# A two-layer hybrid decoder trunk in fp32 on one core: transposes at the borders of the MLP handed out as deferred work, and the opening rebuilt

## The chip, the core and the metric

The kernel runs on one core of a Trainium2 chip. The core has a matrix engine (TensorE, PE in the profile; its weight loads are PEld), a vector engine (VectorE, DVE), a scalar engine (ScalarE, ACT), GpSimd (POOL) and a sync engine (SP) that here only issues transfers. Each engine works through its own instructions in their program order and waits at an instruction until what that needs is there. The metric is device time in microseconds (us), less is better. A change of under 0.2% (5 us) can hardly be told from none here.

## The reference

Two layers over h, 256 rows (tokens) by 2048:

```
u = rms_norm(h, norm_mix_pre);  proj = u @ w_in
mix = concat(nsa_mixer(...), rglru_mixer(...), gla_mixer(...))
h = h + rms_norm(mix @ w_out, norm_mix_post)
u = rms_norm(h, norm_mlp_pre)
h = h + rms_norm(square(relu(u @ w_up)) @ w_down, norm_mlp_post)
h = h + sigmoid(h @ w_ple_gate) * (p[i] @ w_ple)
```

## The kernel before

**Two words for one fp32 number.** Every fp32 product is made of three passes over rounded operands. `split` makes the two words: ScalarE rounds to `hi` (CAST), VectorE makes the rest, `lo` = x - hi. A product is then `uh*wh + uh*wl + ul*wh`, in this order in `form_a`; so the first two passes of a block need only the hi word of the activations and the third needs their lo word, which VectorE makes.

**Weights** come as a stream of units of 512 KB, each 128x1024 in SBUF. `ensure(i)` issues the transfer of unit i into one of four `raw` buffers and splits it into one of eight `hi`/`lo` pairs; the products call it NBUF = 8 units ahead, so their code puts one `lo<-raw,hi` on VectorE for every unit used.

**Activations** are multiplied in transposed form. `to_t` transposes a 128x512 block on TensorE, four 128x128 pieces into one bank of the two-bank ring `tr`, and splits the bank in two halves into two units of the tile set `u` (ScalarE `u<-tr`, then VectorE `u<-tr,u`, twice). The 256 rows are two halves, hf = 0 and 1, with four blocks m of 512 columns each.

**Projections** run in `form_a` (activations stationary, both halves share the weight units; with grp = 4 it takes four units for hf 0, then the same four for hf 1) or `form_b` (weights stationary). When a half is finished, its evacuation function runs (`ev_o2`, `ev_dn`, ...).

**Borders.** Two per layer matter here. At the *up border* the last block of the output projection (`o2`, n = 3) is evacuated: norm, `h` updated (`stt`, L153), multiplied by the gain of the next norm into `t` (L153 too), transposed into `u2`. Products of `ple(0)` and `ple(1)` follow (12 each, they need no norm), then `up`, which reads `u2`. At the *gate border* the last block of `w_down` (`dn`, r = 3, n = 3) is evacuated the same way, without the gain, into `u3`; `ple(2)`, `ple(3)` follow, then `pg`, which reads `u3`. The rsqrt of a norm is a `pow` on POOL (L298).

**Order.** A scheduler decides the order on each engine; `tc.high_priority()` puts instructions ahead, `tc.issue_after(x)` puts them behind x. `self.bg` holds generators of background work: `pump` advances them as products are issued, `later` is a transposition that waits for some us of products, `flush` and `drain` run them to their end.

**Opening** (`run`). The gain of the first norm is spread over 128 partitions by four products with a row of ones into four PSUM banks (`gbc`); VectorE multiplies each block of x by it, and then it is transposed. `vw` and `vs` are the first two projections, `c` the third; two small transposes of a gate input `z` (L504) stand ahead of `c`.

Of the kernel before, what the change touches and what calls it, by code (L numbers as in the profile page):

```python
# [10 lines left out]
F32 = mybir.dt.float32  # L11
# [7 lines left out]
P = 128  # L19
D = 2048  # L20
T = 256
# [10 lines left out]
NBUF = 8  # L32
# [68 lines left out]
class Trunk:  # L101
    def __init__(self, ctx, tc, a, depth, dbg=None):
        self.tc, self.nc, self.a, self.depth, self.dbg = tc, tc.nc, a, depth, dbg
        self.n = 0
        pool = lambda name, **k: ctx.enter_context(tc.tile_pool(name=name, bufs=1, **k))
        self.sb = pool("sb")
        self.ps = pool("ps", space=PSUM)
        self.cst()
        self.stream = []
        self.loaded = []  # L110
        self.bg = []
        self.nrm = [None, None]
        self.par = []
        self.credit = 0.0


# [33 lines left out]
        self.nc.vector.tensor_tensor(out, a, b, op=op)  # L150

    def stt(self, out, a, s, b, op0=ALU.mult, op1=ALU.add):
        self.nc.vector.scalar_tensor_tensor(out, a, s, b, op0=op0, op1=op1)  # L153

    def ts(self, out, a, s1, s2=None, op0=ALU.mult, op1=ALU.add):
        if s2 is None:
# [24 lines left out]
    def ensure(self, i):  # L181
        nc = self.nc
        while len(self.loaded) <= min(i, len(self.stream) - 1):
# [18 lines left out]
                self.split(hv[:, :, 256:320], lv[:, :, 256:320], gz)  # L202
            self.loaded.append((hi, lo))

    def pump(self, us):
# [20 lines left out]
    def form_a(self, base, nu, k0, ut, evac, grp=1, kpu=2, w=512, ring=None, pre=None):  # L226
        accs = [(ring or self.acc)() for _ in range(2)]
        self.ensure(base)
        for g in range(0, nu, grp):
            us = range(g, min(nu, g + grp))  # L230
            for hf in range(2):
                if hf and g == 0 and pre:
                    pre()
                for u in us:
                    self.ensure(base + u)
                    hi, lo = self.loaded[base + u]
                    for k in range(kpu):
                        kt = k0 + kpu * u + k
                        uh, ul = ut.get(kt, hf * 128, hf * 128 + 128)
                        wh, wl = hi[:, k * w:k * w + w], lo[:, k * w:k * w + w]  # L240
                        last = u == nu - 1 and k == kpu - 1
                        o = accs[hf][:, 0:w]
                        self.mm(o, uh, wh, u == 0 and k == 0, False)
                        self.mm(o, uh, wl, False, False)
                        self.mm(o, ul, wh, False, last)
                    if hf:
                        self.ensure(base + u + NBUF)
                    self.pump(0.72 * kpu * w / 1024)
                if g + grp >= nu:
                    evac(hf, accs[hf])  # L250
# [51 lines left out]
        j = self.t2()  # L302
        self.actf(j, src, AF.Square, accum_out=dst)

    def to_t(self, src, n, hf, ut):
# [3 lines left out]
        bv = b.rearrange("p (k t) -> p k t", k=4)  # L309
        sl = slice(hf * 128, hf * 128 + 128)  # L310
# [5 lines left out]
    def later(self, us, src, n, hf, ut):  # L316
        while us > 0:
            us -= 1.3
            yield 1.3
        self.to_t(src, n, hf, ut)  # L320

    def flush(self):
        for g in list(self.bg):
# [139 lines left out]
    def layer(self, i, ut):  # L463
# [6 lines left out]

        rf = self.rfac
        self.form_a(B("vw"), 4, 0, ut, lambda hf, acc: self.actf(v[:, hf, 1], acc[:, 0:256], AF.Copy, scale=rf(0, hf)),
                    4 if i else 2, 4, 256, pre=self.flush)
        if i == 0:
            self.cst2()
        gt = self.st([P, 2, 48], "gt", 1)
# [21 lines left out]
                    self.rr[:, None, 0:2, None].to_broadcast([P, 8, 2, 4]))  # L498
            self.rrow()
        self.slr = slr  # L500
        gzt = self.st([16, T], "gzt", 1)
# [6 lines left out]
        kcu = self.unit()  # L508
        kc = kcu.rearrange("p (s c t) -> p s c t", s=2, c=2)
        for x in range(2):  # L510
            self.form_b(B("c", x), 4, ut, None, dst=kcu[:, x * 512:x * 512 + 512])
        self.params(rows)
        cm = {}
        self.bg.append(self.compress(kcu, kc, wk, cm))
# [132 lines left out]
        def finish_norm():  # L647


# [25 lines left out]
        for r in range(4):  # L675
            hid = self.new_ut()
            for c in range(4):
                def ev_up(b, t):
                    self.stt(t, t, 0.0, t, op0=ALU.max, op1=ALU.mult)
                    u = hid.u[2 * c + b]  # L680
                    self.split(u[:, :, 0], u[:, :, 1], t.rearrange("p (k t) -> p k t", k=2))
                if r == 0 and c == 0:
                    def ev_up0(hf, acc):
                        rl, sq = self.t2(), self.t2()
                        self.actf(rl, acc, AF.Relu)
                        self.tt(sq, rl, rl)
# [10 lines left out]
            for n in range(4):  # L697
                def ev_dn(hf, acc):
# [3 lines left out]
                    elif r < 3:  # L702
                        self.tt(yc, acc, yc, ALU.add)
                    else:
                        with self.tc.high_priority():
                            post(hf, n, acc, gpost, y, ss)
                            if n == 3:
                                rs = self.rstd(ss[hf], epsc[hf])
                                for m in range(4):
                                    h = self.h[hf][m]  # L710
                                    self.stt(h, self.col(y[hf], m), rs, h)
# [34 lines left out]
                if n == 3:  # L746
                    self.pre_norm(hf, ss[hf])
        for n in range(4):
            self.form_a(B("pg", n), 8, 0, u3, ev_pg, GRP if n in (0, 3) else 1)
        return None if last else u4  # L750


# [400 lines left out]
    def run(self):  # L1153
# [3 lines left out]
        ut = self.new_ut()  # L1157


        ones = self.sb.tile([1, P], F32, name="ones")  # L1160
        self.nc.vector.memset(ones, 1.0)
        gbc = [self.sc(), self.sc(), self.acc(), self.acc()]
        for k in range(2):
            row = self.unit()[0:1]
            self.nc.scalar.dma_start(row, a["norm_mix_pre"][0:1, k * 1024:k * 1024 + 1024])
            for n in range(2):
                self.mm(gbc[2 * k + n], ones, row[:, n * 512:n * 512 + 512], True, True)
        both = []
        for hf in range(2):
            for n in range(4):  # L1170
                self.dma(self.h[hf][n], a["x"][0, hf * 128:hf * 128 + 128, n * 512:n * 512 + 512])
            if hf == 0:
                self.dma(self.id_, a["cst"][:, C_ID:C_ID + P])

            with ExitStack() as q:
                for b in both:
                    q.enter_context(self.tc.issue_after(b.ins))
                for n in range(4):
                    t = self.t2()
                    self.tt(t, self.h[hf][n], gbc[n])  # L1180
                    both = self.to_t(t, n, hf, ut)
                ss = self.sm(4)
                for n in range(4):
                    self.sumsq(self.h[hf][n], ss[:, n:n + 1])
            with self.tc.issue_after(both[0].ins), self.tc.issue_after(both[1].ins):
                self.ensure(2 * hf)
                both = self.parts
                self.ensure(2 * hf + 1)
            self.pre_norm(hf, ss)
        for i in range(self.depth):  # L1190
            ut = self.layer(i, ut)

# [32 lines left out]
```

## Time and profile before

| | |
|---|---|
| median of three runs | 2486.48 us (2484.9 to 2487.35) |
| the profiled execution | 2484.42 us, span 2482.6 us |
| TensorE busy | 2461.9 us (99% of the span) |
| VectorE, ScalarE busy | 1535.0 us (62%), 1289.7 us (52%) |
| transfers | 451.15 MB, mean 182 GB/s |

TensorE is the engine that sets the time; the other engines matter where TensorE waits for them.

### The profile page before, as it was taken

Reading aid. Unit: us, or ns where it says so; the run is one execution under the profiler, and the core shown is the slowest. Engines: PE = TensorE matmul, PEld = TensorE weight load, DVE = VectorE, ACT = ScalarE, POOL = GpSimd, SP = SyncE. Lnnn points to the kernel's source line nnn. Section 1 sums busy time; section 2 is a strip of 40 time slices with the busy share of each in tenths; the row PEclk is TensorE's granted clock in tenths of the full one; section 3 lists DMA queues with packets and bytes.
Section 4 is the critical chain, followed back from the end, with each engine's and each line's share of the span. In section 5 each row is a group of like instructions: output and inputs, shape, how many; then the busy total and the mean of one; then the engine's idle time right before and its main releaser. Section 6 shows DMA issues by size and latency. Waiting matters only on the chain.

```text
span 2482.6 us, 33799 instructions
## 1 busy us (share of the span) xinstructions
PE 2461.9 (99%) x12962; PEld 2081.8 (84%) x12962; DVE 1535.0 (62%) x2123; ACT 1289.7 (52%) x2002; POOL 29.7 (1%) x42
## 2 busy tenths in 40 slices
PE   8999999999999999999999999999999999999999
PEld 7888888888888888888888788888888888888887
DVE  5776767754555555656657767676546546555564
ACT  5686655554443443445556866655544434444452
POOL 0000000000000000000000000000000000000000
PEclk9999999999999999999999999999999999999999
DMA  7644446656656656565675445456566565565653
GB/s 229 194 139 136 141 165 200 188 185 195 191 190 193 189 188 196 190 206 184 193 201 166 131 139 160 156 186 204 188 196 189 191 194 188 189 194 190 207 186 120
DMA packets 286086, 451.15 MB, mean 182 GB/s; under 512 B 32955, under 2 KB 107715, under 8 KB 285925
## 3 DMA queue, kind: packets, MB, share of 16 engines
q1 hardware_dynamic: 285920, 448.98, 56.7%
q8 instruction: 102, 1.67, 0.3%
q14 instruction: 60, 0.48, 0.1%
q10 hardware_dynamic: 4, 0.01, 0.0%
HBM read 446.84 MB, written 2.10 MB: 181 GB/s over the span
## 4 chain that ended last, share of the span: by engine, by line
PE 94%; DVE 2%; ACT 2%; DMA 1%; issue 0%; POOL 0%; SPq 0%; DVEq 0%; ACTq 0%
PE acc L164 63%; PE sc L164 15%; PE tr L164 14%; PE tr L916 1%; PE tr L308 1%; DMA raw<-in_w_in_dram 1%; ACT t L161 1%; DVE lo L147 1%; ACT hi L147 1%; POOL sm L298 0%; DVE u L150 0%; DVE h L153 0%; DVE u L153 0%; DMA raw<-in_w_up_dram 0%; DVE t L153 0%
## 5 line engine op out<-in xcount | busy, mean ns | idle before, releaser
L147 DVE TENSOR_TENSOR lo<-raw,hi 128x1024 fp32r<-128x1024 f32 (+1 forms) x832 | 1007.4, 1213 | 792.1 <-ACT hi L147 787.3
L147 ACT CAST hi<-raw 128x1024 fp32r<-128x1024 f32 (+1 forms) x832 | 866.4, 1043 | 987.1 <-PE acc L164 578.2
L164 PE MATMUL acc<-hi,u 128*128 128x512 f32 (+2 forms) x2944 | 902.2, 384 | 3.5 <-ACT hi L147 3.4
L164 PEld LDWEIGHTS acc<-hi,u 128*128 128x128 f32 x2944 | 547.6, 189 | 109.0 <-ACT hi L147 4.0
L164 PE MATMUL acc<-lo,u 128*128 128x512 f32 (+2 forms) x1472 | 563.5, 383 | 1.4 <-DVE lo L147 1.4
L164 PE MATMUL acc<-u,hi 128*128 128x512 f32 x1920 | 491.3, 395 | 0.0
L164 PEld LDWEIGHTS acc<-u,hi 128*128 128x128 f32 x1920 | 344.4, 189 | 65.3 <-issue 3.1
L164 PEld LDWEIGHTS acc<-lo,u 128*128 128x128 f32 x1472 | 277.6, 189 | 52.5 <-DVE lo L147 1.9
L164 PEld LDWEIGHTS acc<-u,lo 128*128 128x128 f32 x1920 | 262.2, 190 | 18.7
L164 PE MATMUL acc<-u,lo 128*128 128x256 f32 x1920 | 269.3, 283 | 0.0
L164 PE MATMUL sc<-u,hi 128*128 128x512 f32 x512 | 139.7, 394 | 0.0
L164 PE MATMUL tr<-u,hi 128*128 128x512 f32 x512 | 137.3, 390 | 0.0
L164 PE MATMUL sc<-hi,u 128*128 128x512 f32 x384 | 119.3, 389 | 0.0
L164 PE MATMUL tr<-hi,u 128*128 128x512 f32 x384 | 119.2, 389 | 0.0
L164 PEld LDWEIGHTS tr<-u,hi 128*128 128x128 f32 x512 | 96.1, 188 | 21.4
L164 PEld LDWEIGHTS sc<-u,hi 128*128 128x128 f32 x512 | 88.5, 190 | 11.9
L164 PEld LDWEIGHTS sc<-u,lo 128*128 128x128 f32 x512 | 78.3, 189 | 9.9
L164 PEld LDWEIGHTS tr<-hi,u 128*128 128x128 f32 x384 | 72.1, 188 | 15.0
L164 PEld LDWEIGHTS sc<-hi,u 128*128 128x128 f32 x384 | 72.1, 188 | 14.8
L164 PE MATMUL tr<-u,lo 128*128 128x256 f32 x512 | 82.3, 283 | 0.0
L164 PE MATMUL sc<-u,lo 128*128 128x256 f32 x512 | 81.3, 282 | 0.0
L161 ACT ACTIVATE t<-sc,sm,slr 128x128 f32<-128x128 f32 (+1 forms) x128 | 63.9, 506 | 22.0 <-DVE sm L150 22.0
(195 smaller groups left out, 1753.7 us busy)
## 6 DMA issues: line engine op xcount, KB each, us to landing
raw<-in_w_up_dram SPq DMA_DIRECT2D x256, 512.0 KB
raw<-in_w_down_dram SPq DMA_DIRECT2D x256, 512.0 KB
raw<-in_w_in_dram SPq DMA_DIRECT2D x168, 512.0 KB
raw<-in_w_out_dram SPq DMA_DIRECT2D x64, 512.0 KB
raw<-in_w_ple_gate_dram SPq DMA_DIRECT2D x64, 512.0 KB
raw<-in_w_in_dram SPq DMA_DIRECT2D x16, 256.0 KB
raw<-in_w_ple_dram SPq DMA_DIRECT2D x8, 512.0 KB
h<-in_x_dram SPq DMA_DIRECT2D x8, 256.0 KB
```

The costliest lines, as they stand in the source:

```text
L147: return self.nc.scalar.copy(hi, src), self.nc.vector.tensor_sub(lo, src, hi.bitcast(F32))
L161: self.nc.scalar.activation(out, a, f, **k)
L164: self.last = self.nc.tensor.matmul(out, l, r, start=start, stop=stop, skip_group_check=True)
L308: self.nc.tensor.transpose(b[:, k * 128:k * 128 + 128], src[:, k * 128:k * 128 + 128], self.ident)
L916: nc.tensor.transpose(b[:, x * 128:x * 128 + 128], pe[:, x * 128:x * 128 + 128], self.ident)
```

## The change

1. **Opening.** The gain is loaded as 16 rows of 128, transposed once, and used as a scalar for each partition after the transposition, so x is transposed as it lands; the four products with ones go. The transposes of the second half become background work between the first products; its sums of squares stand behind the splits of units 2 and 3. Two products without use stand ahead of the first projection.
2. **Up and gate border.** The transposes of both halves are no longer issued in the evacuation function, with its high priority, but handed to `later`. `until` finishes those of hf 0 ahead of the first product that reads them, `flush` those of hf 1 inside `form_a`. After the first `stt` of a half, the next four calls of `ensure` are issued behind it (`hold`, `fetch`).
3. **`z`.** Its two transposes and their copy stand behind the products of `c`.

```
+    def fetch(self, i):
+        if not self.hold:
+            self.ensure(i)
+            return
+        with self.tc.issue_after(self.hold[0]):
+            self.ensure(i)
...
-                        self.ensure(base + u + NBUF)
+                        self.fetch(base + u + NBUF)
...
+    def until(self, ut):
+        for g, u in self.due:
+            if u is ut:
+                self.drain(g)
+        self.due = []
...
-                        self.stt(h, self.col(y[hf], m), r, h)
+                        q = self.stt(h, self.col(y[hf], m), r, h)
+                        if m == 0:
+                            self.hold = [q.ins, 4]
                         t = self.t2()
                         self.stt(t, h, nr[:, 1:2], self.col(gpre, m), op0=ALU.mult, op1=ALU.mult)
-                        self.to_t(t, m, hf, u2)
+                        self.bg.append(self.later(1.3 if m else 3.9, t, m, hf, u2))
...
-                    self.form_a(B("up", r, c), 8, 0, u2, ev_up0, GRP)
+                    self.until(u2)
+                    self.form_a(B("up", r, c), 8, 0, u2, ev_up0, GRP, pre=self.flush)
...
-                                    self.to_t(h, m, hf, u3)
+                                    self.bg.append(self.later(1.3 if m else 2.6, h, m, hf, u3))
...
-        gbc = [self.sc(), self.sc(), self.acc(), self.acc()]
...
+        g16, gt = self.unit()[0:16, 0:P], self.sm(16)
+        self.nc.scalar.dma_start(self.id_, a["cst"][:, C_ID:C_ID + P])
+        self.nc.scalar.dma_start(g16, a["norm_mix_pre"][0].rearrange("(k p) -> k p", p=P))
+        b = self.tr()
+        self.nc.tensor.transpose(b[:, 0:16], g16, self.ident[0:16, 0:16])
+        self.nc.vector.tensor_copy(gt, b[:, 0:16])
...
+                    both = self.to_t(self.h[0][n], n, 0, ut, gt[:, 4 * n:4 * n + 4])
...
+                hi = self.loaded[0][0]
+                for _ in range(2):
+                    self.mm(self.sc(), hi[:, 0:P], hi[:, 0:512], True, True)
...
+        def other():
+            for n in range(4):
+                with self.tc.issue_after(first[0].ins), self.tc.issue_after(first[1].ins), \
+                        self.tc.issue_after(self.last.ins):
+                    self.both = self.to_t(self.h[1][n], n, 1, ut, gt[:, 4 * n:4 * n + 4])
+                yield 0.7
+        self.bg.append(other())
```

**What moves on VectorE at the up border of layer 0.** The rows are instructions in their order on the engine, `out<-in`; `h_65` to `h_68` are the blocks of hf 0 and `h_69` to `h_72` those of hf 1, `t_` their multiples by the gain, `lo_` weights, `u_..<-tr_` the lo word of a transposed block. Line numbers are those of the program listed (L153 before is L155 after, L147 is L149). Before, the first split of a transposed block is the sixth row from the first `h`:

```order
L153 SCALAR_TENSOR_TENSOR h_65<-u_3497,sm_4196,h_65 128x512
L153 SCALAR_TENSOR_TENSOR h_66<-u_3497,sm_4196,h_66 128x512
L153 SCALAR_TENSOR_TENSOR t_4202<-h_65,nrm_166,u_3904 128x512
L150 TENSOR_TENSOR u_3500<-acc_4167,u_3500 128x512
L153 SCALAR_TENSOR_TENSOR t_4214<-h_66,nrm_166,u_3904 128x512
L147 TENSOR_TENSOR u_3910<-tr_4204,u_3910 128x2x128
```

On the same engine after the change, the same split is the 26th row from the first `h`. Here are the last twelve of these:

```order
L160 TENSOR_SCALAR sm_4261<-sm_4262 128x1
L149 TENSOR_TENSOR lo_4253<-raw_4251,hi_4252 128x1024
L155 SCALAR_TENSOR_TENSOR h_69<-u_3495,sm_4261,h_69 128x512
L155 SCALAR_TENSOR_TENSOR h_70<-u_3495,sm_4261,h_70 128x512
L155 SCALAR_TENSOR_TENSOR t_4267<-h_69,nrm_269,u_3900 128x512
L155 SCALAR_TENSOR_TENSOR t_4270<-h_70,nrm_269,u_3900 128x512
L155 SCALAR_TENSOR_TENSOR h_71<-u_3496,sm_4261,h_71 128x512
L155 SCALAR_TENSOR_TENSOR h_72<-u_3496,sm_4261,h_72 128x512
L155 SCALAR_TENSOR_TENSOR t_4273<-h_71,nrm_269,u_3901 128x512
L155 SCALAR_TENSOR_TENSOR t_4276<-h_72,nrm_269,u_3901 128x512
L149 TENSOR_TENSOR lo_4299<-raw_4297,hi_4298 128x1024
L149 TENSOR_TENSOR u_3906<-tr_4303,u_3906 128x2x128
```

The 14 rows ahead of these are the eight `h` and `t` of hf 0, three weight splits, and three of the norm of hf 1 (`u_3496<-acc`, its product with the gain, the sum); so the split of hf 0 has moved behind everything that hf 1 does on this engine.

On TensorE at the same place, after the change, `tr_4334` is the transposition of block 1, `acc_4376` the first half of `up`, and the third product, with the lo word of `u_3906`, is the first of the two in the row marked x2:

```order
L166 MATMUL acc_4314<-hi_4113,t_3474 128x512
L321 MATMUL tr_4334<-ident,t_4201 128x128 x4
L166 MATMUL acc_4376<-hi_4131,u_3906 128x512
L166 MATMUL acc_4376<-lo_4132,u_3906 128x512
L166 MATMUL acc_4376<-hi_4131,u_3906 128x512 x2
L166 MATMUL acc_4376<-lo_4132,u_3906 128x512
L321 MATMUL tr_4358<-ident,t_4204 128x128 x4
L166 MATMUL acc_4376<-hi_4131,u_3906 128x512
L321 MATMUL tr_4367<-ident,t_4207 128x128 x4
L166 MATMUL acc_4376<-hi_4153,u_3907 128x512
```

Before, all four transposes of hf 0 stood among the 24 products of `ple` and the first three of `up`; now two of them stand among the products of `up` that read the blocks before them.

**VectorE at the gate border of layer 0.** Before, the first split of a transposed block is the fourth row from the first `h`:

```order
L153 SCALAR_TENSOR_TENSOR h_65<-u_4402,sm_9936,h_65 128x512
L153 SCALAR_TENSOR_TENSOR h_66<-u_4402,sm_9936,h_66 128x512
L153 SCALAR_TENSOR_TENSOR h_67<-u_4403,sm_9936,h_67 128x512
L147 TENSOR_TENSOR u_9364<-tr_9942,u_9364 128x2x128
L153 SCALAR_TENSOR_TENSOR h_68<-u_4403,sm_9936,h_68 128x512
```

After, it is the 17th; the twelve rows that follow `h_65` to `h_68` and `lo_9949` end with it:

```order
L152 TENSOR_TENSOR u_4347<-acc_9831,u_4347 128x512
L149 TENSOR_TENSOR lo_9961<-raw_9959,hi_9960 128x1024
L152 TENSOR_TENSOR u_4347<-u_4347,u_9357 128x512
L305 TENSOR_REDUCE sm_10003<-sm_4349 128x1
L149 TENSOR_TENSOR lo_9973<-raw_9971,hi_9972 128x1024
L160 TENSOR_SCALAR sm_10002<-sm_10003,epsc_3915 128x1
L149 TENSOR_TENSOR lo_9985<-raw_9983,hi_9984 128x1024
L155 SCALAR_TENSOR_TENSOR h_69<-u_4346,sm_10002,h_69 128x512
L155 SCALAR_TENSOR_TENSOR h_70<-u_4346,sm_10002,h_70 128x512
L155 SCALAR_TENSOR_TENSOR h_71<-u_4347,sm_10002,h_71 128x512
L155 SCALAR_TENSOR_TENSOR h_72<-u_4347,sm_10002,h_72 128x512
L149 TENSOR_TENSOR u_9360<-tr_9989,u_9360 128x2x128
```

Here too the split of hf 0 has moved behind the four `h` of hf 1. Layer 1 has the same order at both borders.

**TensorE in the opening.** Before (`sc_83` to `acc_86` are the gain, `tr_` the transposes of hf 0, `acc_256` the first half of `vw`):

```order
L164 MATMUL sc_83<-u_87,ones 128x512
L164 MATMUL sc_84<-u_87,ones 128x512
L164 MATMUL acc_85<-u_91,ones 128x512
L164 MATMUL acc_86<-u_91,ones 128x512
L308 MATMUL tr_102<-ident,t_100 128x128 x4
L308 MATMUL tr_113<-ident,t_111 128x128 x4
L308 MATMUL tr_124<-ident,t_122 128x128 x4
L308 MATMUL tr_135<-ident,t_133 128x128 x4
L164 MATMUL acc_256<-hi_154,u_73 128x256
```

After:

```order
L1201 MATMUL tr_85<-ident,u_81 128x16
L321 MATMUL tr_95<-ident,h_65 128x128 x4
L321 MATMUL tr_108<-ident,h_66 128x128 x4
L321 MATMUL tr_121<-ident,h_67 128x128 x4
L321 MATMUL tr_134<-ident,h_68 128x128 x4
L166 MATMUL sc_157<-hi_146 128x512
L166 MATMUL sc_159<-hi_146 128x512
L166 MATMUL acc_178<-hi_146,u_73 128x256
```

The gain no longer stands ahead of the transposes; the eight transposes of two blocks of hf 1 follow after 12 products of `acc_178`, the other eight after 12 more, and only then its second half.

## Rows read from the trace of the kernel before

**Rows 1.** Page, part 1: busy us of each engine, share of the span, instructions

```profile
PE 2461.9 (99%) x12962; PEld 2081.8 (84%) x12962; DVE 1535.0 (62%) x2123; ACT 1289.7 (52%) x2002; POOL 29.7 (1%) x42
```

**Rows 2.** Waits of TensorE: for whom, us in total, times, longest

```profile
PE tr L504 <- DVE sm L157: 2.1, 2, 1.3
...
PE tr L308 <- DVE t L153: 1.0, 2, 0.5
PE tr L308 <- DVE h L153: 0.9, 2, 0.5
```

**Rows 3.** Timeline of TensorE in the opening: start, us, instruction, count, idle before

```profile
2.38 3.75 PE L164 MATMUL sc<-u,ones 1*128 1x512 f32 x4 [2.38 <-DMA u<-in_norm_mix_pre_dram]
...
12.48 1.09 PE L308 MATMUL tr<-ident,t 128*128 128x128 f32 x4 [1.04 <-DVE u L147]
...
18.86 0.58 PE L164 MATMUL acc<-lo,u 128*128 128x256 f32 x1 [0.68 <-DVE lo L147]
...
21.81 0.63 PE L164 MATMUL acc<-hi,u 128*128 128x256 f32 x2
22.23 0.41 PE L164 MATMUL acc<-lo,u 128*128 128x256 f32 x1
...
24.23 0.41 PE L164 MATMUL acc<-hi,u 128*128 128x256 f32 x2
24.47 0.28 PE L164 MATMUL acc<-lo,u 128*128 128x256 f32 x1
...
26.93 0.63 PE L308 MATMUL tr<-ident,t 128*128 128x128 f32 x4
...
31.54 0.39 PE L164 MATMUL acc<-lo,u 128*128 128x256 f32 x1 [0.76 <-DVE lo L147]
```

**Rows 4.** Timeline of ScalarE and VectorE in the opening

```profile
3.46 0.63 ACT L161 ACTIVATE t<-h 128x512 f32<-128x512 f32 x1 [0.65 <-DMA h<-in_x_dram]
...
16.64 0.42 DVE L147 TENSOR_TENSOR u<-tr,u 128x256 fp32r<-128x256 f32 x1 [0.44 <-ACT u L147]
...
19.86 1.28 DVE L150 TENSOR_TENSOR t<-h,sc 128x512 f32<-128x512 f32 x2
```

**Rows 5.** Granted clock of a stretch of the opening: us, busy by engine, clock, DMA share, GB/s

```profile
21.00:22.40 1.40, 1.40 (x8) 1.40 (x8) 0.73 (x2) 0.00 (x0) 0.00 (x0) 1.00 0.64 189
```

**Rows 6.** Timeline of VectorE at the up border of layer 0

```profile
434.77 1.42 DVE L153 SCALAR_TENSOR_TENSOR h<-u,sm,h 128x512 f32<-128x512 f32 x2 [0.44 <-POOL sm L298]
436.10 0.75 DVE L153 SCALAR_TENSOR_TENSOR t<-h,nrm,u 128x512 f32<-128x512 f32 x1
436.76 0.68 DVE L150 TENSOR_TENSOR u<-acc,u 128x512 f32<-128x512 f32 x1
...
438.06 0.42 DVE L147 TENSOR_TENSOR u<-tr,u 128x256 fp32r<-128x256 f32 x1
...
441.42 1.22 DVE L147 TENSOR_TENSOR lo<-raw,hi 128x1024 fp32r<-128x1024 f32 x1
442.56 0.41 DVE L147 TENSOR_TENSOR u<-tr,u 128x256 fp32r<-128x256 f32 x1
```

**Rows 7.** Timeline of TensorE and ScalarE at the same border

```profile
434.27 0.62 PE L164 MATMUL acc<-hi,u 128*128 128x512 f32 x2
...
436.08 0.39 PE L164 MATMUL sc<-lo,t 128*128 128x512 f32 x1
...
436.99 0.63 PE L308 MATMUL tr<-ident,t 128*128 128x128 f32 x4 [0.52 <-DVE t L153]
...
437.37 0.70 PE L164 MATMUL sc<-hi,t 128*128 128x512 f32 x2
...
438.52 0.88 ACT L147 CAST u<-tr 128x256 fp32r<-128x256 f32 x2 [0.49 <-DVE u L147]
```

**Rows 8.** Timeline at the gate border of layer 0, TensorE and VectorE

```profile
1151.09 0.39 PE L164 MATMUL acc<-lo,u 128*128 128x512 f32 x1
...
1151.14 2.08 DVE L153 SCALAR_TENSOR_TENSOR h<-u,sm,h 128x512 f32<-128x512 f32 x3 [0.44 <-POOL sm L298]
```

More of the change, by code (lines that the diff above doesn't have):

```diff
@@ L113, in __init__ @@
         self.par = []
+        self.hold = []
+        self.due = []
         self.credit = 0.0
@@ L152, in stt @@
     def stt(self, out, a, s, b, op0=ALU.mult, op1=ALU.add):
-        self.nc.vector.scalar_tensor_tensor(out, a, s, b, op0=op0, op1=op1)
+        return self.nc.vector.scalar_tensor_tensor(out, a, s, b, op0=op0, op1=op1)
     def ts(self, out, a, s1, s2=None, op0=ALU.mult, op1=ALU.add):
@@ L203, in ensure @@
             self.loaded.append((hi, lo))
+    def fetch(self, i):
[4 more added lines that the diff above has]
+            self.ensure(i)
+        self.hold[1] -= 1
+        if not self.hold[1]:
+            self.hold = []
     def pump(self, us):
@@ L303, in sumsq, with to_t @@
         self.actf(j, src, AF.Square, accum_out=dst)
[L305 removed]
+    def to_t(self, src, n, hf, ut, gt=None):
         b = self.tr()
@@ L309, in to_t @@
         bv = b.rearrange("p (k t) -> p k t", k=4)
+        if gt is not None:
+            t = self.t2().rearrange("p (k t) -> p k t", k=4)
+            self.tt(t, bv, gt[:, :, None].to_broadcast([P, 4, P]))
+            bv = t
         sl = slice(hf * 128, hf * 128 + 128)
@@ L316, in later, with wait_then @@
     def later(self, us, src, n, hf, ut):
+        g = self.wait_then(us, src, n, hf, ut)
+        if hf == 0:
+            self.due.append((g, ut))
+        return g
+    def wait_then(self, us, src, n, hf, ut):
         while us > 0:
@@ L500, in layer @@
         self.slr = slr
+        kcu = self.unit()
+        kc = kcu.rearrange("p (s c t) -> p s c t", s=2, c=2)
+        for x in range(2):
+            self.form_b(B("c", x), 4, ut, None, dst=kcu[:, x * 512:x * 512 + 512])
         gzt = self.st([16, T], "gzt", 1)
@@ L505, in layer @@
         nc.scalar.copy(gzt, b[0:16, 0:T])
[L508 to L511, printed above, removed]
         self.params(rows)
@@ L710, in ev_dn @@
                                     h = self.h[hf][m]
-                                    self.stt(h, self.col(y[hf], m), rs, h)
-                                    self.to_t(h, m, hf, u3)
+                                    q = self.stt(h, self.col(y[hf], m), rs, h)
+                                    if m == 0:
+                                        self.hold = [q.ins, 4]
+                                    self.bg.append(self.later(1.3 if m else 2.6, h, m, hf, u3))
                 self.form_a(B("dn", r, n), 8, 0, hid, ev_dn, GRP if r == 3 and n == 3 else 1,
@@ L1157, in run @@
         ut = self.new_ut()
-        ones = self.sb.tile([1, P], F32, name="ones")
-        self.nc.vector.memset(ones, 1.0)
-        gbc = [self.sc(), self.sc(), self.acc(), self.acc()]
[L1163 to L1168, printed above, removed]
+        g16, gt = self.unit()[0:16, 0:P], self.sm(16)
[4 more added lines that the diff above has]
+        self.nc.vector.tensor_copy(gt, b[:, 0:16])
         for hf in range(2):
@@ L1172, in run, with before @@
             if hf == 0:
[L1173 to L1181, printed above, removed]
                 ss = self.sm(4)
                 for n in range(4):
[L1184 to L1189, printed above, removed]
+                    self.sumsq(self.h[0][n], ss[:, n:n + 1])
+                    both = self.to_t(self.h[0][n], n, 0, ut, gt[:, 4 * n:4 * n + 4])
+                with self.tc.issue_after(both[0].ins), self.tc.issue_after(both[1].ins):
+                    self.ensure(0)
+                    first = self.parts
+                    self.ensure(1)
+                hi = self.loaded[0][0]
+                for _ in range(2):
+                    self.mm(self.sc(), hi[:, 0:P], hi[:, 0:512], True, True)
+                self.pre_norm(0, ss)
+        def other():
[5 more added lines that the diff above has]
+        self.bg.append(other())
+        def before():
+            self.flush()
+            with self.tc.issue_after(self.both[0].ins), self.tc.issue_after(self.both[1].ins):
+                self.ensure(3)
+            ss = self.sm(4)
+            with self.tc.issue_after(self.parts[0].ins):
+                for n in range(4):
+                    self.sumsq(self.h[1][n], ss[:, n:n + 1])
+            self.pre_norm(1, ss)
+            self.pre = self.flush
+        self.pre = before
         for i in range(self.depth):
```

7 lines of the change are left out of this document (5 added, 2 removed).

## The prediction

> **What bounds the kernel now.** First the page: TensorE is busy for 2461.9 of 2482.6 us [rows 1], so the time is what TensorE has to do plus where it waits. Its waits, the second view, are few; of those that the change touches, the two small transposes of `z` wait 2.1 us for VectorE, and the first transposition at each of the four borders about half a microsecond, 1.9 us together [rows 2]. Only the opening is loose: TensorE's first product in three words with a lo operand starts at 18.86 us, and units 2 and 3 at 31.54 us [rows 3]. So at the borders there are 1.9 us to be won and much to be lost: what matters there is whether what now hides the work of VectorE still does. The third view is therefore the timeline of VectorE and TensorE at a border [rows 6, 7, 8], read beside the new order of instructions.
>
> **The up border, twice.** VectorE's order there decides. Now it gives the first transposed block its lo word at 438.06, 3.3 us after the first `h` at 434.77 [rows 6], and TensorE goes on. After the change the same split stands behind 25 instructions, counted in the order shown with the change: 16 `h` and `t` of both halves, five weight splits, two blocks of the norm of hf 1, its sum and its scale. Their price is the step from one start to the next. Two `h` start at 434.77 and the `t` behind them at 436.10, so 0.665 each, and `t` takes 0.66 to the next row. A weight split takes 442.56 - 441.42 = 1.14. The block from `acc` lasts 0.68 and overlaps its successor as the `h` do, 0.08, so 0.60; its product with the gain the same; sum and scale together I take as 0.2 (bounds 0.1 and 0.4) [rows 6]. Sum: 16 x 0.665 = 10.6, 5 x 1.14 = 5.7, 1.2 and 0.2, in all 17.7. VectorE starts at 434.77 as now, since the first `h` waits for POOL's `pow` in both [rows 6], and so begins the first split at 452.5; with its 0.42 the lo word is there at 452.9. Nothing shorter is possible while the engine keeps its order; a wait within the chain would only lengthen it. The norm's second `pow` fits in under a weight split.
>
> TensorE arrives much earlier. Eight products start between 434.27 and 436.08, so 0.227 each; four transposes cost 437.37 - 436.99 = 0.38 [rows 7]. `ple` begins at 435.85, one product ahead of 436.08. 24 products and two transpositions later, 5.45 + 0.76, it is at 442.06; the first two products of `up` need only the hi word; the third needs the lo word, at 442.5. **Wait: 452.9 - 442.5 = 10.4 us.** Everything on TensorE stands behind it, the later transposes too.
>
> Two smaller waits follow. The transposition of block 2 needs the bank of block 0, which is free once both its halves are split. ScalarE's second cast waits for VectorE's first split (it does so now: 0.49 us, [rows 7]), a weight split stands ahead of VectorE's second, so the bank is free at 452.9 + 1.14 + 0.4 less overlap, 454.35, against TensorE's arrival at 453.55: 0.8. For block 3 the bank of block 1 takes two evacuations of `ple` on ScalarE and four alternating splits at 0.4: 455.8 against 454.95: 0.9. The splits of hf 1 then keep up. In exchange the wait of 0.5 at the first transposition goes [rows 7]. Net 10.4 + 0.8 + 0.9 - 0.5 = 11.6 a border, 23.2 for two layers.
>
> The edit `hold`, which lets four weight splits go behind the first `h`, costs nothing by itself: those units are used only much later. It is the transposes moved out of the high priority that let the splits of hf 0 fall behind hf 1.
>
> **The gate border, twice.** The first `h` starts at 1151.14 and three start within 2.08 us [rows 8]. Ahead of the first split now stand eight `h` (no `t` here), four weight splits, the two blocks, sum and scale: 8 x 0.665 + 4 x 1.14 + 1.2 + 0.2 = 11.3; lo word at 1151.14 + 11.3 + 0.42 = 1162.9. TensorE: from 1151.09 five products to the end of `dn`, a transposition, 12 products, a transposition, 12 products, two of `pg`: 31 x 0.227 + 0.76 = 7.8, so 1158.9. **Wait: 4.0.** Banks behind it cost perhaps 0.3; 0.5 goes [rows 2]. Net 3.8, for two layers 7.6.
>
> **The opening.** What goes: four products of the gain, from 2.38 on [rows 3], which hold up the multiplication of x; VectorE's product of x (0.64 a block, [rows 4]) remains, now behind the transposition. The first block lands by 3.46 [rows 4]; four transposes take 1.09 at the opening's pace [rows 3]; then VectorE needs about 0.64 + 2 x 0.42 = 1.5 a block [rows 4], so four end at 3.46 + 1.09 + 6.0 = 10.6. From the start of the last split but one, 16.64, to the first product with a lo operand it is now 2.2 us [rows 3, 4]; VectorE also waits for the `pow` of the norm, 0.5 by estimate. That puts this product near 13.2 instead of 18.86: 5.7 earlier. The second half: 24 products and 16 transposes follow, 24 x 0.21 + 4 x 1.09 = 9.4 at the low pace and 24 x 0.12 + 4 x 0.38 = 4.4 at the high one; from the last four transposes to the first lo operand of unit 2 it is 31.54 - 26.93 = 4.6 [rows 3]. So unit 2 starts between 22 and 27, taken 25.5 instead of 31.54: **-6.0** (bounds -7 and -4; a late gain or identity, now on ScalarE's queue, would take some back). The two idle products lie in the wait for the lo word. The sums of squares of hf 1 and the changed order of small transfers lie beside the 5 us of products of units 2 and 3.
>
> **`z`.** The wait of 2.1 goes [rows 2]; behind `c` its operands are long there. **-2.1** (bounds -2.1 and 0, if weights are late next).
>
> **TensorE's clock.** The granted clock reads 1.00 even in the opening [rows 5], but the same 128x256 product starts every 0.21 us up to 22.4 and every 0.12 from 24.2 on [rows 3]: the lower and the higher of the two levels (1.2 and 2.4 GHz). The engine had run products without a gap from 18.86 before it rose, some 3.5 to 5.3 us, while the four products from 2.38 on and the transposes had not raised it. No row shows a fall after the opening, as no wait there is longer than the 1.3 at `z` [rows 2]; a wait of 10.4 is nearer to the idle opening than to those. If it falls, the engine runs 4.4 us at 0.21 instead of 0.12: 4.4 x (1 - 0.12 / 0.21) = 1.9 lost. I take this for the two long waits, 3.8, and not for the two of 4.0 (bounds 0 and 7.6).
>
> The Trainium skill has a rule against this change ("TensorE: Matmul & The Clock Gate", section "Why this matters for your kernels"): idle gaps between bursts of matmuls put the clock back to the low level. By it the sum has the 3.8, and more if it holds for the shorter waits; by the rows of before alone it would be without. Its section "Part 4: PE-mode transpose" says that transposes do not count as work for the clock; the opening's pace, low behind 16 of them, agrees.
>
> **Sum.** 23.2 + 7.6 - 6.0 - 2.1 + 3.8 = +26.5. The profiled execution took 2484.42 us (span 2482.6), so 2510.9; the median of the runs is 2.06 above it, so **2513 us**, 1.1% slower.
>
> **Rivals.**
> (a) *The clock holds.* The waits are there, the clock stays high: 2509. For it: no fall in the rows. Chance 0.27.
> (b) *The clock falls at all four waits, or the opening gains less.* +3.8, and up to 2 + 2 from opening and `z`: 2517 to 2521. For it: a wait of 4.0 is three times any that the clock is seen to survive. Chance 0.16.
> (c) *Faster.* The lo word of the first block comes before TensorE's third product of `up`. It decides at 442.5: VectorE would need the 25 instructions and the split in 7.7 us, 0.3 each, or the split would have to stand earlier. Then 1.9 more is won and nothing lost: 2486.5 - 6.0 - 2.1 - 1.9 = 2476.5. Against it: the shortest large row there lasts 0.68. Chance 0.07.
> (d) *A wash.* The waits are a third of what I work out, as if half of VectorE's rows went under TensorE's: 2484 to 2489. Chance 0.04.
>
> **How the numbers follow.** The forecast, 2513, has 0.46; with (a) and (b) 0.89. The range takes in these three with the bounds of opening, `z` and the small waits: 2503 to 2521. Slower by over 0.2% (5 us, about what can be told from no change): 0.46 + 0.27 + 0.16 less a little for errors of mine that share a cause, 0.88; faster by over 0.2%: (c), 0.07; within: 0.05.
>
> **What would show it.** TensorE at both up borders idle for some 10 us at the third product of `up`, released by VectorE's split of a transposed block, and 4 us at `pg`; VectorE without a gap between the first `h` and that split; its first split at 17.7 and 11.3 us from the first `h`; the first products after the long wait at 0.4 instead of 0.227; units 2 and 3 of the opening near 25.5; no wait at `z`. I am wrong if VectorE reaches the split early, or if the opening gains 20 us, which nothing in it could.

## The result and the profile after

The changed kernel takes 2508.32 us (median of four runs, 2508.24 to 2511.12) against 2485.69 (2483.91 to 2487.35) for the one before: ratio 1.0091, 95% interval 1.0079 to 1.0103. It is slower by 22.6 us; the forecast was 2513, with a range of 2503 to 2521. The profiled execution took 2508.34 us, 23.9 more than that of before.

TensorE's waits in the trace after, the view of [rows 2] (for whom, us in total, times, longest):

```profile
PE acc L166 <- DVE u L149: 25.3, 4, 9.5
PE tr L1201 <- DMA u<-in_norm_mix_pre_dram: 4.7, 1, 4.7
PE sc L166 <- ACT hi L149: 2.5, 1, 2.5
PE tr L166 <- ACT t L841: 1.3, 1, 1.3
...
```

The first row is new: four waits for VectorE's split of a transposed block, one at each border. The waits at `z` and at the borders' first transpositions [rows 2] are gone, and one of 1.3 in the compression (L841 is ScalarE's copy of `t` there) has come that nobody had asked for.

TensorE at the up border of layer 0, the counterpart of [rows 7]:

```profile
436.01 0.40 PE L166 MATMUL acc<-lo,u 128*128 128x512 f32 x1
445.88 1.22 PE L166 MATMUL acc<-hi,u 128*128 128x512 f32 x2 [9.48 <-DVE u L149]
446.90 0.63 PE L166 MATMUL acc<-lo,u 128*128 128x512 f32 x1
447.44 1.09 PE L321 MATMUL tr<-ident,t 128*128 128x128 f32 x4
448.18 0.78 PE L166 MATMUL acc<-hi,u 128*128 128x512 f32 x1
448.95 1.09 PE L321 MATMUL tr<-ident,t 128*128 128x128 f32 x4
...
451.49 0.62 PE L166 MATMUL acc<-hi,u 128*128 128x512 f32 x2
451.95 0.39 PE L166 MATMUL acc<-lo,u 128*128 128x512 f32 x1
```

TensorE stands for 9.48 us at the third product of `up`. Behind that, two products take 1.02 from start to start (445.88 to 446.90) and not the 0.46 of 451.49 to 451.95. Why it stands there is on VectorE, the counterpart of [rows 6]:

```profile
427.27 1.42 DVE L155 SCALAR_TENSOR_TENSOR h<-u,sm,h 128x512 f32<-128x512 f32 x2 [0.66 <-POOL sm L311]
428.60 1.41 DVE L155 SCALAR_TENSOR_TENSOR t<-h,nrm,u 128x512 f32<-128x512 f32 x2
...
437.31 1.22 DVE L149 TENSOR_TENSOR lo<-raw,hi 128x1024 fp32r<-128x1024 f32 x1
438.97 1.41 DVE L155 SCALAR_TENSOR_TENSOR h<-u,sm,h 128x512 f32<-128x512 f32 x2 [0.44 <-POOL sm L311]
...
444.27 1.22 DVE L149 TENSOR_TENSOR lo<-raw,hi 128x1024 fp32r<-128x1024 f32 x1
445.41 0.42 DVE L149 TENSOR_TENSOR u<-tr,u 128x256 fp32r<-128x256 f32 x1
```

The first split begins 445.41 - 427.27 = 18.1 us behind the first `h`; 17.7 were forecast. Its 0.42 end at 445.83, and TensorE goes on at 445.88.

The gate border of layer 0 on TensorE and VectorE, the counterpart of [rows 8]:

```profile
1163.74 0.39 PE L166 MATMUL acc<-lo,u 128*128 128x512 f32 x1
1167.28 0.89 PE L166 MATMUL acc<-hi,u 128*128 128x512 f32 x2 [3.15 <-DVE u L149]
...
1168.38 1.06 PE L166 MATMUL acc<-hi,u 128*128 128x512 f32 x2
...
1171.50 0.63 PE L166 MATMUL acc<-hi,u 128*128 128x512 f32 x2
```

```profile
1155.04 2.74 DVE L155 SCALAR_TENSOR_TENSOR h<-u,sm,h 128x512 f32<-128x512 f32 x4 [0.67 <-POOL sm L311]
...
1166.80 0.42 DVE L149 TENSOR_TENSOR u<-tr,u 128x256 fp32r<-128x256 f32 x1
```

TensorE's granted clock in stretches around both borders (columns: the stretch, its length, busy us of PE, PEld, VectorE, ScalarE and POOL, PEclk, DMA share, GB/s):

```profile
430.00:435.00 5.00, 5.00 (x26) 4.14 (x25) 5.00 (x8) 2.91 (x6) 0.00 (x0) 1.00 0.06 10
436.40:445.80 9.40, 0.00 (x1) 0.00 (x0) 8.96 (x14) 2.09 (x2) 1.46 (x1) 0.73 0.56 185
445.90:450.60 4.70, 4.70 (x14) 3.42 (x15) 3.21 (x7) 3.08 (x8) 0.00 (x0) 0.50 0.70 205
451.00:455.00 4.00, 4.00 (x21) 3.30 (x20) 0.42 (x1) 0.32 (x1) 0.00 (x0) 1.00 0.01 3
1163.90:1167.20 3.30, 0.23 (x1) 0.00 (x0) 3.05 (x6) 1.04 (x1) 0.21 (x1) 1.00 0.75 240
1167.30:1171.40 4.10, 4.10 (x13) 3.34 (x14) 3.28 (x5) 2.79 (x7) 0.00 (x0) 0.58 0.63 219
```

After the wait of 9.48 the clock is at 0.50, the lower level, for 4.7 us; after that of 3.15 its mean is 0.58 over 4.1 us. It falls at the shorter wait too, and at both borders of layer 1 (0.50 from 1688.9 to 1693.2 and from 2410.2 to 2413.5).

The opening, the counterpart of [rows 3]:

```profile
4.65 0.26 PE L1201 MATMUL tr<-ident,u 16*128 16x16 f32 x1 [4.65 <-DMA u<-in_norm_mix_pre_dram]
...
14.11 0.58 PE L166 MATMUL acc<-lo,u 128*128 128x256 f32 x1 [0.52 <-DVE lo L149]
...
16.41 0.41 PE L166 MATMUL acc<-hi,u 128*128 128x256 f32 x1
...
18.12 0.40 PE L166 MATMUL acc<-hi,u 128*128 128x256 f32 x2
...
24.49 0.39 PE L166 MATMUL acc<-lo,u 128*128 128x256 f32 x1 [0.76 <-DVE lo L149]
```

The first lo product of units 2 and 3 starts at 24.49 instead of 31.54.

**Where the time went.** One looks up the same product in both traces and subtracts the starts: that is how far TensorE is ahead (-) or behind (+).

| place | before | after | difference | step |
|---|---|---|---|---|
| first lo product of unit 2 | 31.54 | 24.49 | -7.05 | opening -7.05 |
| compression, 16 products into a `tr` bank | 117.87 | 109.80 | -8.07 | `z`, layer 0: -1.02 |
| 8 products of hi words behind it | 125.63 | 119.12 | -6.51 | **given back +1.56** |
| transposes of `p`, before up | 342.12 | 335.69 | -6.43 | |
| MLP, 8 lo products | 501.41 | 506.31 | +4.90 | up border +11.33 |
| products of `pg` | 1200.08 | 1209.43 | +9.35 | gate border +4.45 |
| parameters, layer 1 | 1302.99 | 1310.89 | +7.90 | `z`, layer 1: -1.45 |
| MLP, layer 1 | 1745.70 | 1765.30 | +19.60 | up border +11.7 |
| end | 2482.6 | 2506.5 | +23.9 | gate border +4.3 |

### The profile page after: what moved, and what is told of

It reads as the page before. It is cut to its first block, busy times and chain, and to the rows that moved or that the text cites. A ratio compares the mean times of both kernels' runs of the same rounds, so it can differ in the third digit from the quotient of the medians.

```text
span 2506.5 us, 33804 instructions
## 1 busy us (share of the span) xinstructions
PE 2463.2 (98%) x12957; PEld 2085.4 (83%) x12957; DVE 1537.0 (61%) x2123; ACT 1290.3 (51%) x2002; POOL 29.2 (1%) x42
## 4 chain that ended last, share of the span: by engine, by line
PE 94%; DVE 3%; ACT 1%; issue 1%; POOL 0%; DMA 0%; POOLq 0%; SPq 0%; ACTq 0%; DVEq 0%
PE acc L166 63%; PE tr L166 14%; PE sc L166 14%; DVE lo L149 1%; PE tr L953 1%; PE tr L321 1%; DVE h L155 1%; ACT t L163 1%; ACT hi L149 0%; DVE t L155 0%; DVE u L152 0%; POOL sm L311 0%; DVE u L155 0%; DVE t L152 0%; DVE u L149 0%
## 5 line engine op out<-in xcount | busy, mean ns | idle before, releaser
L149 DVE TENSOR_TENSOR lo<-raw,hi 128x1024 fp32r<-128x1024 f32 (+1 forms) x832 | 1007.7, 1213 | 787.5 <-ACT hi L149 779.8
L149 ACT CAST hi<-raw 128x1024 fp32r<-128x1024 f32 (+1 forms) x832 | 866.4, 1043 | 984.1 <-PE acc L166 564.0
L166 PE MATMUL acc<-hi,u 128*128 128x512 f32 (+2 forms) x2944 | 906.2, 386 | 25.3 <-DVE u L149 25.3
```

The source lines that it names most:

```text
L149: return self.nc.scalar.copy(hi, src), self.nc.vector.tensor_sub(lo, src, hi.bitcast(F32))
L166: self.last = self.nc.tensor.matmul(out, l, r, start=start, stop=stop, skip_group_check=True)
```

## The experiments

**1. The deferral undone, whole or at one border.**

```diff
-  self.bg.append(self.later(1.3 if m else 3.9, t, m, hf, u2))   # ev_o2, in high priority
+  self.to_t(t, m, hf, u2)
-  self.bg.append(self.later(1.3 if m else 2.6, h, m, hf, u3))   # ev_dn, in high priority
+  self.to_t(h, m, hf, u3)
```

Both: 

> The changed kernel with its transpositions at the up and gate borders handed out at once again, inside the high priority, while hold, the opening and z stay as changed. Theory (VectorE's order at the borders is what costs): the two up borders cost 11.3 each and the two gate borders 4.5 each in the changed kernel, so 31.6 us go: 2508.3 - 31.6 = 2476.7, 0.3% faster than before; no wait above 1.5 us for VectorE's split of a transposed block. Rival (the weight splits held behind the first h cost by themselves): four splits of 1.14 us stand behind the h at each of four borders, and where they come late TensorE waits for lo: 4.6 x 4 = 18 us of the loss stay, about 2495.

Measured: 2477.51 (2476.44 to 2478.98), ratio to before 0.9968 [0.9956, 0.9981]. Faster than before, and no wait for a split is left. So the whole loss sits in the borders. In TensorE's waits of this kernel the first row below is the wait in the compression, which has grown; the other two are all that waits at the borders now:

```profile
PE tr L166 <- ACT t L841: 1.7, 1, 1.7
...
PE tr L321 <- DVE t L155: 1.2, 2, 0.6
...
PE tr L321 <- DVE h L155: 0.7, 2, 0.4
```

Up alone: 

> The changed kernel with the transpositions of the up border alone handed out at once. Theory: the two up borders give back 11.3 each: 2508.3 - 22.6 = 2485.7, with the two waits of 3.2 at the gate left. Rival (one border's delay is partly made up at the next): less than 22.6 comes back, as what is late at up is hidden elsewhere: 2490 or more.

Gate alone: 

> The changed kernel with the transpositions of the gate border alone handed out at once. Theory: 4.5 come back at each of two borders: 2508.3 - 9.0 = 2499.3, with the two waits of 9.5 at up left. Rival (the low clock behind the gate's wait is no part of its price): only the waits of 3.2 come back: 2501.9.

Measured, one execution each: 2487.68 and 2501.18, so 20.7 and 7.2 come back, not 22.6 and 9.0. By time alone the 7.2 are nearer to the 6.4 of the rival at the gate; the traces decide. Much of what is short is lost ahead of the borders: the openings are ahead by 6.3 and 6.2 where the changed kernel's trace had 7.05, and between the 16 products of the compression and the transposes of `p` 2.6 and 2.9 are given back instead of 1.6. Of these, 1.6 each lie in a stretch behind the compression in which the granted clock reads 0.50 (first with up direct, then with the gate direct); in the changed kernel it reads 1.00 there:

```profile
125.50:128.80 3.30, 3.30 (x13) 2.91 (x13) 1.98 (x4) 1.49 (x2) 0.00 (x0) 0.50 0.33 82
```

```profile
125.80:129.10 3.30, 3.30 (x13) 2.91 (x13) 2.08 (x4) 1.45 (x2) 0.00 (x0) 0.50 0.29 69
```

At the borders themselves, read as in the table above, the direct gates cost 0.2 and 0.1 instead of 4.45 and 4.3, so about 8.4 come back there: the low clock is part of the gate's price, and the rival is out. Direct up borders cost nothing (-0.2 and 0.0). The borders left as they were cost 11.6 and 10.7 at up and 5.5 and 4.0 at the gate, so their price holds to about 1 us.

**2. The deferral kept, the priority given back.**

```diff
     def wait_then(self, us, src, n, hf, ut, hp=False):
         ...
-        self.to_t(src, n, hf, ut)
+        if hp:
+            with self.tc.high_priority():
+                self.to_t(src, n, hf, ut)
+        else:
+            self.to_t(src, n, hf, ut)
...
-                        self.bg.append(self.later(1.3 if m else 3.9, t, m, hf, u2))
+                        self.bg.append(self.later(1.3 if m else 3.9, t, m, hf, u2, True))
...
-                                    self.bg.append(self.later(1.3 if m else 2.6, h, m, hf, u3))
+                                    self.bg.append(self.later(1.3 if m else 2.6, h, m, hf, u3, True))
```

> The changed kernel, with the transpositions still deferred, but traced inside the high priority when they are handed out, so that the first split of a transposed block stands 12 instructions behind the first h on VectorE instead of 25. Theory (the priority, not the deferral, costs): the lo word is there about 8 us after the first h, 435.5 at the up border, before TensorE's third product at 436.2: the waits of 9.5 and 3.2 go and so do the half-microsecond waits of before: 2475 to 2477. Rival (the splits pushed ahead only move the wait): the h and t of the second half now stand behind eight splits of 0.42, 3.4 us later, and TensorE waits for the second half instead, up to 3.4 at each border: 2477 + 13.6 = 2490.

Measured: 2478.86 (2476.86 to 2481.89), ratio 0.9973 [0.9962, 0.9984]. VectorE at its up border of layer 0:

```profile
426.82 1.42 DVE L155 SCALAR_TENSOR_TENSOR h<-u,sm,h 128x512 f32<-128x512 f32 x2 [0.66 <-POOL sm L311]
...
434.59 0.42 DVE L149 TENSOR_TENSOR u<-tr,u 128x256 fp32r<-128x256 f32 x1
...
436.65 0.75 DVE L155 SCALAR_TENSOR_TENSOR h<-u,sm,h 128x512 f32<-128x512 f32 x1 [0.44 <-POOL sm L311]
```

The split comes 7.8 us behind the first `h`, in front of the second half's `h`, and TensorE passes its third product without a wait. The priority alone turns 2508 into 2479: its loss was the cause, not the deferral. But the 1.9 us of short waits did not go either: rows of 1.2, 0.7 and 0.8 stand in their place (for `t`, `h` and `u`). The up border of layer 0 costs 0.7 more than before (342.12 to 335.24, then 501.41 to 495.22). So deferring is worth nothing here even in the right order; the rival's 13.6 did not come.

**3. `hold` undone** (`fetch` calls `ensure` and nothing else). 

> The changed kernel with hold alone undone: the four weight splits are no longer queued behind the first h; the transpositions stay deferred. Theory (hold costs nothing by itself): VectorE's first split of a transposed block now stands 24 instructions behind the first h instead of 25, one weight split less (1.14 us), which goes ahead of the h and delays them by some 0.5: the waits at up stay near 9 and those at gate near 3: 2505 to 2508. Rival (the weight splits past the scaling are what makes TensorE wait): four of 1.14 go at each of four borders, 18 us: 2490.

Measured, one execution: 2508.05, with the waits as they were (first row of TensorE's waits):

```profile
PE acc L166 <- DVE u L149: 24.8, 4, 9.4
```

`hold` is neutral, and the two timelines say why: without it a weight split goes ahead of the `h`, which start at 428.00 instead of 427.27 while TensorE is 0.33 earlier, so 1.1 later against TensorE; with it that split, 1.14, stands behind them, ahead of the transposed block. That the weight splits past the scaling cost by themselves is refuted.

**4. Idle products in the long wait.** In `form_a` of the first `up`, behind its second product:

```diff
                         self.mm(o, uh, wl, False, False)
+                        if fill and not (hf or u or k):
+                            idle = self.sc()
+                            with self.tc.issue_after(self.last.ins):
+                                for _ in range(fill):
+                                    self.mm(idle, uh, wl, True, True)
+                            with self.tc.issue_after(self.last.ins):
+                                self.mm(o, ul, wh, False, last)
+                            continue
                         self.mm(o, ul, wh, False, last)
...
-                    self.form_a(B("up", r, c), 8, 0, u2, ev_up0, GRP, pre=self.flush)
+                    self.form_a(B("up", r, c), 8, 0, u2, ev_up0, GRP, pre=self.flush, fill=40)
```

> The changed kernel with 40 idle products of 128x512 between the second and the third product of up at both up borders, some 9.1 us in the wait of 9.5; the gate border stays as changed, for comparison. Their result is not used. Theory (the clock falls for the long idle time, and with it the products behind the wait start every 0.43 instead of 0.227): now they start every 0.227 from the third on, and what is left is the wait for banks; the wait and what follows to the steady pace get shorter by 0.5 to 1.5 at each up border: 2505.3 to 2507.3. At the gate the spacing stays 0.43 for some 4 us. Rival (the spacing behind the wait is the pace of the splits, not the clock): it stays 0.4 at up too, and the time 2508.

Measured, one execution: 2506.03. TensorE at the up border, then the granted clock there and behind the unfilled gate wait of the same run:

```profile
438.08 9.25 PE L166 MATMUL sc<-lo,u 128*128 128x512 f32 x40
447.73 0.74 PE L166 MATMUL acc<-hi,u 128*128 128x512 f32 x2 [0.40 <-DVE u L149]
448.31 0.40 PE L166 MATMUL acc<-lo,u 128*128 128x512 f32 x1
...
449.29 0.63 PE L329 MATMUL tr<-ident,t 128*128 128x128 f32 x4 [0.35 <-DVE u L149]
```

```profile
448.00:452.00 4.00, 3.65 (x20) 2.79 (x20) 2.80 (x7) 2.73 (x8) 0.00 (x0) 1.00 0.70 218
...
1168.00:1171.00 3.00, 3.00 (x11) 2.40 (x10) 2.48 (x5) 1.69 (x6) 0.00 (x0) 0.53 0.57 185
```

Busy instead of idle, the clock stays at 1.00, and the border costs 501.41 to 506.20 less 342.12 to 337.53, +4.79 + 4.59 = 9.4 instead of 11.3: the low clock is worth 1.9 there, more than the 0.5 to 1.5 expected. (The transpositions of the third and fourth block also moved, by one and five products.) The second up border costs 9.6 instead of 11.7. Of the 4.1 won the time shows 2.3, since this kernel gave back 1.8 more than the changed one ahead of the border, with the clock at 0.50 from 117.2 to 120.2. The gate, left as it was, still reads 0.53.

**5. Opening alone, `z` alone.** Each is that part of the diff on the kernel before.

Opening: 

> The kernel before with the new opening alone; z, borders and hold as before. Theory: 6.2 to 7.1 us won by units 2 and 3; TensorE then runs ahead of weights and of VectorE, and 1.3 to 2.9 come back as a wait in the compression of the first layer (TensorE's product of t, released by ScalarE's copy), where the kernel before has none: net -4 to -5.5 against the kernel before, 2480.5 to 2481.5. Rival (that wait belongs to the moved z): no such wait here, net -6.2 to -7.1, about 2479.

`z`: 

> The kernel before with z's transposition behind c alone. Theory: the two waits of 0.84 and 1.26 go with the gaps around them, 1.0 and 1.45, and nothing comes back: -2.5 against the kernel before, 2483.2; no wait in the compression of the first layer. Rival (the moved z makes the new wait there): 1.3 or more of it comes back, 2484.5.

Measured: 2478.63, ratio 0.9968 [0.9957, 0.9979]; and 2482.59, ratio 0.9986 [0.9976, 0.9996]. With `z` alone nothing comes back, as the theory had it. With the opening alone the time is the rival's, 2479, and there is no wait in the compression, as it said; but its reason, that nothing comes back, is not what the trace shows. This row of TensorE's waits is at layer 0's `z`, where before waited 0.84:

```profile
PE tr L534 <- DVE sm L159: 2.1, 1, 2.1
```

The 16 products of the compression start at 113.70 instead of 117.87: 4.2 are left of 7.0. The wait is 1.3 longer than before; most of the rest lies in the stretch right behind it, at the lower clock:

```profile
48.20:51.50 3.30, 3.30 (x14) 2.73 (x13) 1.81 (x4) 1.53 (x4) 0.00 (x0) 0.50 0.99 254
```

So what is given back belongs to the opening; it shows as a longer wait at an early dependence and as a low clock behind it. What makes the time good again is layer 1's wait of 1.26 at `z`, which is gone in this kernel though `z` was not moved: there ScalarE waited 2.78 for a weight in the trace of before, and here less than 0.9. It is gone in experiment 6's kernel too, where neither `z` nor the opening is changed, so that half of the `z` term cannot be booked to `z`: other changes bring it as well, and why stays open. The parts do not add up: -7.1 and -3.1 alone, -8.1 together (experiment 1); the 1.4 of layer 1 are in both.

**6. Borders alone** (deferral and `hold` on the kernel before). 

> The kernel before with the deferred transpositions and hold alone; opening and z as before. Theory (the parts hardly touch one another): two up borders at 11.3 and two gate borders at 4.5, so 2484.4 + 31.6 = 2516.0. Rival (the borders' price depends on how far the opening brought TensorE ahead): the price differs from that by 2 or more, 2514 or 2518.

Measured, one execution: 2517.51, 33.1 above the profiled execution of before, 1.5 more than the theory. The surplus is not at the borders: the four waits sum to 25.2 (25.3 in the changed kernel), and the up border of layer 0 costs 11.55 (342.12 to 344.46, then 501.41 to 515.30); the four borders together cost 32.1. TensorE is already 2.3 late ahead of the first: 0.9 at layer 0's `z`, whose wait is 1.8 here instead of 0.84, and 1.5 behind the compression, where the clock reads 0.50. At layer 1's `z` nothing waits (the row counts one wait), which takes 1.5 off again:

```profile
PE tr L534 <- DVE sm L159: 1.8, 1, 1.8
```

```profile
132.60:135.90 3.30, 3.30 (x12) 2.92 (x13) 1.94 (x4) 1.44 (x2) 0.00 (x0) 0.50 0.35 78
```

So the borders' price does not depend on the opening, and the rival's 2518 is near for another reason than its own.

**7. What comes back of the opening.** On experiment 1's kernel with both borders direct, the loads of the compression's weights are moved down in `layer`:

```diff
-  for kv in range(2): self.dma(wk[kv]..., a["nsa_cmp_w"]...)      # behind vs
   ...
+  for kv in range(2): self.dma(wk[kv]..., a["nsa_cmp_w"]...)      # behind c and z
   self.bg.append(self.compress(kcu, kc, wk, cm))
```

> The kernel of e1_direct_both with the two transfers of the compression's weights (512 KB each, wanted only some 50 us later) queued behind six to seven units of c's weights, instead of ahead of c's second half. Theory (what comes back of the opening's gain in the first layer, 2.9 us in e1, comes from weights that land late behind those transfers): the weights land some 5 us earlier, the wait at the copy of t is below 0.5 and 1.3 to 2.9 come on top: 2474.6 to 2476.2. Rival (VectorE and ScalarE are late there for their own work): nothing, 2477.5.

Beside it: 

> The kernel of e1_direct_both once more beside e10, on the same chip: 2477.5, and 1.3 to 2.9 above e10 by the theory given there, no difference by its rival.

Measured: 2476.57 (2476.3 to 2480.36), ratio 0.9965 [0.9953, 0.9977], against 2478.23 (median of six runs, one of them a stray 11293; the next highest is 2479.2), ratio 0.9967 [0.9955, 0.9979]. The runs alone do not part the two. The traces do: the transposition behind the copy, first with the loads late, then with them early:

```profile
116.54 0.43 PE L166 MATMUL tr<-cst,t 128*128 128x64 f32 x2 [0.92 <-ACT t L841]
```

```profile
117.39 0.43 PE L166 MATMUL tr<-cst,t 128*128 128x64 f32 x2 [1.64 <-ACT t L841]
```

From the 16 products (110.28 and 110.39, so 7.59 and 7.48 ahead) to the 8 products behind (119.21 and 121.40, 6.42 and 4.23 ahead) 1.2 us come back instead of 3.3. Of the 2.1 between them, 0.7 are the shorter wait; the rest comes behind it, where the granted clock parts the two (late, then early):

```profile
116.60:121.70 5.10, 5.10 (x30) 4.50 (x31) 2.80 (x4) 3.48 (x12) 0.00 (x0) 1.00 0.65 207
```

```profile
118.60:121.70 3.10, 3.10 (x13) 2.81 (x12) 0.01 (x1) 2.41 (x8) 0.00 (x0) 0.50 0.89 293
```

That the late loads did this is not shown. In the changed kernel and those of experiments 2 and 3, which load early and whose clock stays at 1.00 there, only 1.56, 1.29 and 1.25 come back over the same stretch, after waits of 1.31, 1.02 and 0.99: hardly more than the 7.59 - 6.42 = 1.17 with late loads. So the size of what comes back goes with the clock. The wait did not fall below 0.5 as the theory had it, and neither theory nor rival is settled. By the median this is the fastest kernel of the study; its lead over before is shown, that over experiment 1's kernel is not.

## Why the prediction was right

**The order on VectorE: right.** The 25 instructions stood where they were counted and took 18.1 us (17.7 forecast; the 0.44 is the norm's second `pow`, which was to fit in under a weight split and did not).

**Up, wait of 10.4: 9.48.** The price of VectorE was right and TensorE's arrival was not: it would be at its third product at 436.01 + 0.23 = 436.24, so 436.24 - 427.27 = 9.0 from the first `h`, not 7.7. The step that failed is "VectorE starts at 434.77 as now": with `hold` the `h` begin 1.1 earlier against TensorE (experiment 3). One weight split more behind them takes the 1.1 back, so `hold` costs nothing, as forecast, for a reason that was not seen.

**What follows the wait: 3.6 forecast (banks 0.8 + 0.9, clock 1.9), 2.35 measured** (11.33 - 9.48 + 0.5). Experiment 4, where the low clock is taken out, gives 1.9 and 2.1 for the clock's 1.9. The banks were over-priced, and the two terms were added as if they lay behind one another: at the low clock TensorE reaches the next transposition at 447.44, when the bank is already free (VectorE's second split ends at 447.30), and with the clock kept high it waits 0.35. So up gave 11.33 + 11.7 instead of 27.0.

**Gate, 7.6: 4.45 + 4.3.** The wait was 3.15 rather than 4.0: VectorE took 1166.80 - 1155.04 = 11.8 (11.3 forecast), but TensorE would have been at its third product at 1163.74 + 0.23, so 8.9 behind the first `h` and not 7.8, by the same step as at up. And the clock, which I took to hold there, fell. Of rival (b) the condition came true (the clock falls at all four waits); its time did not, since up was over-priced by 4. Rival (a), that the clock holds, is out. The Trainium skill's rule ("TensorE: Matmul & The Clock Gate", section "Why this matters for your kernels") that idle gaps put the clock back agrees with 0.50 and 0.58 behind the two waits.

**Opening, -6.0: -7.05 at unit 2, -5.5 after the compression.** That TensorE 7 us earlier would wait further on was no term of the sum: the 1.56 are a wait for ScalarE's copy in the compression and what follows it. Other kernels with the same opening gave back up to 3.4 (experiment 4), so that the net is so near to -6.0 is in part luck. The gain's landing on ScalarE's queue took some back, as a bound said: TensorE's first transposition waits for it until 4.65, where 3.46 was forecast, and the first lo product is at 14.11, not 13.2. (In that sum 16.64 [rows 4] is the start of the last split of hf 0, not of the last but one; read so, it gives about 12.9.)

**`z`, -2.1: -1.02 - 1.45 = -2.5**, of which the 1.45 at layer 1 come without moving `z` too (experiments 5 and 6): the sum is near, but only layer 0's half can be put down to this edit.

Together: 23.0 + 8.8 - 5.5 - 2.5 = +23.8 (0.1 lies between the places of the table) against +26.5; errors of -4.0 at up, +1.2 at the gate, +0.5 in the opening and -0.4 at `z` partly cancel.

## What to carry to other kernels

Moving a call out of a high-priority block moves everything that it issues, on every engine: before deferring, count what then stands ahead of its first instruction on each in-order engine, and give the deferred call the priority back. Price a stall at its wait and what follows, but do not add a low clock to waits that it runs under. A gain early in the program is worth what is left of it behind the next waits, and a low clock behind such a wait can take as much as the wait itself; look there before booking it.

## What the runs showed of the hardware

The record of the granted clock reads 0.50 behind the wait of 9.48, where products start at the slow pace, but 1.00 in the opening at the same slow pace [rows 3, 5]: at the start the spacing of products tells the level, and the record does not. Over the wait of 3.15 itself the record reads 1.00, over the wait of 9.48 0.73: behind the shorter one the fall came only once TensorE was running again. The clock also read 0.50 behind shorter waits, of 2.11 (experiment 5) and 1.64 (experiment 7), and in experiments 1 and 6 behind a row of 128x32 products, with no wait above 1.05 in the 10 us ahead; in the changed kernel it stayed at 1.00 through the same products and behind the wait of 1.31. In the opening the spacing of 128x256 products goes from 0.21 at 16.41 to 0.12 at 18.12, some 6 us earlier than before (24.23, [rows 3]), with the two idle products at 12.16 and the first lo product at 14.11 ahead of it.
